# Layer 0 of a hybrid-mixer kernel: the state-space mixer moved behind all projections, beside axial attention

## The chip, the cores and the metric

The kernel runs on one core of a Trainium2 chip. The core has five engines that run at the same time, each with its own queue of instructions that it works through in order: TensorE (matmuls, PE in the profile, with its weight loads as PEld), VectorE (DVE), ScalarE (ACT), GpSimd (POOL) and SyncE (SP, which here only issues DMAs). The metric is the device time of one execution in microseconds, as the median of several runs.

## The reference, cut to what matters

Two layers work on 512 latent and 256 context tokens of width 1024. Each layer projects the normalised tokens once and feeds four parallel mixers; the context is only needed as an output of the first layer (`need_ctx`).

```python
def _layer(x, xc, c, c_ctx, rope, need_ctx, ...):
    ...
    aq, ak, av, dq, dk, dv, fin, sin_ = _split_proj(h @ w_in)
    caq, cak, cav, cdq, cdk, cdv, cfin, csin = _split_proj(hc @ w_in)
    o_a, oc_a = _gqa_mixer(aq, ak, av, caq, cak, cav, att_q_gain, att_k_gain, rope, need_ctx)
    o_d, oc_d = _na_mixer(dq, dk, dv, cdq, cdk, cdv, na_q_gain, na_k_gain, na_rel_bias, need_ctx)
    o_f = _fourier_mixer(fin, w_fourier)
    o_s, oc_s = _s5_mixer(sin_, csin, ssm_lam_re, ssm_lam_im, ssm_log_dt, ..., need_ctx)
    o = _group_norm(jnp.concatenate([o_a, o_d, o_f, o_s.astype(o_a.dtype)], axis=-1), g_group)
    x = x + ga1 * (o @ w_out)
    h2 = _rmsnorm(x, g_norm2) * (1.0 + sc2) + sh2
    x = x + ga2 * _swiglu(h2, w_ff1, w_ff3, w_ff2)
```

`_gqa_mixer` is the axial attention of the change's name (4 heads, rotary positions), `_na_mixer` the near attention (a window with a bias), `_s5_mixer` a state-space scan over the tokens in both directions with a gelu and a gated linear unit at its end.

## The kernel before, in words

The kernel is written in a tile language: the program gives tiles, pools and instructions; a scheduler then orders the instructions of each engine by program order as priority, whether they are ready, and its own clock. An instruction waits for the tiles that it reads and for the release of the space that it writes, be it a buffer of a pool or space that an earlier, closed pool held. SBUF is two stacks: pools opened on the left and on the right (`side="right"`). PSUM has eight banks; in each stage they are given out to roles (`psum_pools`): `D` for dense work, `S` for scores, `Q` for attention's other matmuls, `T` for everything that fills in.

Precision is kept by splitting float32 into a high and a low part: `mm3` (L237) does three matmuls per product, and `weights` (L222) loads a weight group on SP's queue, makes the high part on ScalarE (L231) and the low part on POOL (L232).

`mixers` (L1084) is called once per layer. For layer 0 (l = 0) its program order before the change is:

1. The projections for s5 (`oS`), for the queries and keys of axial attention (`aq`, `ak`), their head statistics, norm and rotary step (L1100 to L1118), in role D, T for the statistics.
2. `before_s5`, which is `tables` (L424): the coefficients of s5, made on VectorE and POOL with small matmuls in role S, stored to DRAM through ScalarE's queue.
3. Inside the pool `s5{l}` (`sp` on the left stack): `s5` (L707) in role S; then the projections DK, DQ (L1126) and V (L1145) in role D.
4. After `sp` is closed: the pools `fo`, `on`, `qk`, `fh` in the same space, the splits `k2`, `q2` of axial attention (L1160), and the F projection (L1170), emptied into `fhi` and `flo` (L1165).
5. The stage `b`, with S = 2 tiles of 1024, Q = 2 and T = 2 banks: `attend` twice (L957), and as fillers in role T `mods_pe` for chunks 4 and 5 (L358), `group_stats` of `oS`, `norm_heads` of near attention, and `fourier` (L829) in a pool `ft` on the left.
6. The stage `c`: near attention (L996), whose bias (`nab`) is loaded on SP's queue (L1197) into the pool `qn`, `mods_pe` for chunks 6 to 9 and the group norms in role T, then the output projection in role D.

`s5` makes two passes (m = 0, 1), each: transposes (L719, L727), a matmul with R per direction (L747), a run of VectorE instructions per direction (L754 to L784, with two scans L765 and the state moves L782, L784), the output matmuls (L799, L801), transposes back (L808) and a gelu (L810). After both, the gated unit: matmuls L819, sigmoid L821, products L827. Its tiles `rr`, `oo`, `toep` share three buffers; the rotation tables `rot` have two. Its loads (R, rot, O, T) are issued on POOL's queue.

`attend` works on blocks of two query tiles: scores (L932) into S, the maximum on VectorE (L972, L973), the exponential on ScalarE (L974), transposes (L979), copies (L982, L984), the values (L990), and the division (L946 to L952).

The pool `ga` of axial attention is opened on the right, where `h`, the input of all projections, was held until the F projection ended.

## Time and profile before

| | us |
|---|---|
| median of three runs | 1827.36 |
| the three runs | 1827.08, 1827.36, 1835.40 |
| the profiled execution, in all | 1835.55 |
| its span, first to last instruction | 1833.8 |
| TensorE busy / VectorE busy / ScalarE busy / POOL busy | 1725.8 / 969.5 / 527.2 / 558.6 |
| mean granted share of TensorE's clock | 0.967 |

All rows are from the one profiled execution; its time is close to the highest of the runs. Times inside a trace are us from the first instruction. Layer 0's mixers lie between about 55 and 440 us of it. A line number is that of the kernel before; a helper's line (L241, L232, L265) stands for all of its callers, and the tile's name tells them apart.

### The profile page before, as it was taken

How to read it: one execution, taken by the hardware profiler on the slowest of the kernel's cores; microseconds unless marked ns; L12 is line 12 of the kernel's file. 1: busy time of each engine (PE TensorE's matmuls, PEld its weight loads, DVE VectorE, ACT ScalarE, POOL GpSimd, SP SyncE). 2: the span in 40 equal slices, each digit the busy share in tenths (PEclk: the TensorE clock that was granted, in tenths of full speed). 3: DMA queues.
4: the chain of work that ended last, by engine and by line, in shares of the span. 5: the costliest groups of instructions: out<-in, count | busy, mean ns of one | idle time of the engine just before them, and what ended most of it. 6: DMA issues, size and time to landing. Idle time of an engine off the chain costs nothing.

```text
span 1833.8 us, 25688 instructions
## 1 busy us (share of the span) xinstructions
PE 1725.8 (94%) x10142; PEld 1395.3 (76%) x10142; DVE 969.5 (53%) x2259; ACT 527.2 (29%) x852; POOL 558.6 (30%) x360
## 2 busy tenths in 40 slices
PE   5899999898999999999899998989999999999999
PEld 2667877566878888888678877778767787787887
DVE  7988535572177445446956346265666632232332
ACT  2422234452241211121121223323444432222221
POOL 4553200201221322231643512423111244344442
PEclk7999989999999999999899998989999999999999
DMA  8355340414135434343342332332322123233222
GB/s 337 103 155 165 128 167 24 167 53 182 38 125 151 127 127 153 107 154 110 106 110 75 106 112 81 132 110 89 114 64 64 47 92 93 77 107 103 93 92 81
DMA packets 83065, 207.25 MB, mean 113 GB/s; under 512 B 15360, under 2 KB 35968, under 8 KB 82816
## 3 DMA queue, kind: packets, MB, share of 16 engines
q1 hardware_dynamic: 54160, 160.44, 26.9%
q0 software_dynamic: 7824, 29.38, 4.8%
q10 hardware_dynamic: 20960, 15.78, 2.8%
q8 instruction: 80, 1.31, 0.3%
q14 instruction: 41, 0.34, 0.1%
HBM read 185.68 MB, written 21.99 MB: 113 GB/s over the span
## 4 chain that ended last, share of the span: by engine, by line
PE 76%; DVE 15%; issue 4%; ACT 2%; POOL 1%; DMA 1%; ACTq 0%; DVEq 0%; POOLq 0%
PE psD L241 54%; PE psD L703 4%; PE psS L932 3%; PE psT L241 2%; PE psQ L979 1%; PE psQ L990 1%; PE psT L376 1%; PE psS L801 1%; POOL lo L232 1%; PE psT L856 1%; PE psQ L1045 1%; DVE ro L662 1%; PE psQ L1030 1%; PE psT L278 1%; PE psT L1067 1%
## 5 line engine op out<-in xcount | busy, mean ns | idle before, releaser
L232 POOL TENSOR_TENSOR lo<-raw,hi 128x1024 fp32r<-128x1024 f32 (+1 forms) x178 | 432.2, 2434 | 875.5 <-ACT hi L231 875.2
L241 PE MATMUL psD<-big,hi 128*128 128x512 f32 (+1 forms) x2368 | 605.9, 360 | 12.2 <-ACT big L331 5.7
L241 PEld LDWEIGHTS psD<-big,hi 128*128 128x128 f32 x2368 | 399.8, 191 | 88.1 <-ACT big L331 8.1
L231 ACT CAST hi<-raw 128x1024 fp32r<-128x1024 f32 (+1 forms) x178 | 184.2, 1039 | 774.5 <-PE psD L241 466.6
L241 PE MATMUL psD<-big,lo 128*128 128x512 f32 (+1 forms) x1184 | 368.2, 359 | 1.2 <-POOL lo L232 1.2
L241 PEld LDWEIGHTS psD<-big,lo 128*128 128x128 f32 x1184 | 202.9, 191 | 38.4 <-POOL lo L232 2.7
L1332 DVE TENSOR_TENSOR sg<-sg,psD 128x768 f32<-128x768 f32 (+1 forms) x44 | 36.1, 820 | 308.8 <-PE psD L241 300.5
L241 PE MATMUL psD<-gh,hi 128*128 128x512 f32 (+1 forms) x528 | 163.6, 359 | 4.9 <-DVE xb L1248 4.7
L241 PE MATMUL psD<-gl,hi 128*128 128x512 f32 (+1 forms) x528 | 165.8, 360 | 0.0
L241 PE MATMUL psD<-gh,lo 128*128 128x512 f32 (+1 forms) x528 | 163.6, 358 | 0.0
L1248 DVE SCALAR_TENSOR_TENSOR xb<-psD,mod,xb 128x512 f32<-128x512 f32 (+1 forms) x112 | 64.7, 613 | 114.9 <-PE psD L241 114.8
L1337 DVE TENSOR_TENSOR gl<-sg,gh 128x768 fp32r<-128x768 f32 (+1 forms) x44 | 99.2, 2254 | 39.5 <-ACT gh L1335 39.5
L407 DVE CUSTOM_DVE_ANT_0 junk<-wmt,cb,pcol 128x1024 f32<-128x1024 f32 x64 | 97.1, 1517 | 27.3 <-DMA wmt<-in_wmodT 26.2
L241 PEld LDWEIGHTS psD<-gh,hi 128*128 128x128 f32 x528 | 89.5, 189 | 24.4 <-DVE xb L1248 8.5
L241 PEld LDWEIGHTS psD<-gh,lo 128*128 128x128 f32 x528 | 90.1, 189 | 16.6 <-issue 0.2
L241 PEld LDWEIGHTS psD<-gl,hi 128*128 128x128 f32 x528 | 89.8, 189 | 15.8 <-issue 0.4
L1248 DVE SCALAR_TENSOR_TENSOR xq<-psD,mod,xq 128x512 f32<-128x512 f32 (+1 forms) x64 | 42.2, 682 | 78.6 <-PE psD L241 78.6
L932 PE MATMUL psS<-k,q 64*128 64x256 f32 (+1 forms) x432 | 78.2, 336 | 3.4 <-DVE mx L1019 3.0
L241 PE MATMUL psD<-h,hi 128*128 128x512 f32 (+1 forms) x288 | 76.2, 350 | 4.2 <-ACT h L331 2.7
L932 PEld LDWEIGHTS psS<-k,q 64*128 64x128 f32 x432 | 58.1, 195 | 23.6 <-issue 9.1
L241 PEld LDWEIGHTS psD<-h,hi 128*128 128x128 f32 x288 | 50.7, 194 | 15.4 <-ACT h L331 3.2
L241 PE MATMUL psD<-on,hi 128*128 128x256 f32 (+1 forms) x176 | 51.6, 331 | 1.3 <-ACT on L1081 1.3
(396 smaller groups left out, 2494.5 us busy)
## 6 DMA issues: line engine op xcount, KB each, us to landing
raw<-in_w_ff SPq DMA_DIRECT2D x132, 512.0 KB, 3.5
wmt<-in_wmodT SPq DMA_DIRECT2D x48, 512.0 KB, 3.6
wm<-in_wmod SPq DMA_DIRECT2D x28, 512.0 KB, 6.0
raw<-in_winT SPq DMA_DIRECT2D x18, 512.0 KB, 3.6
room<-in_wmod SPq DMA_DIRECT2D x12, 512.0 KB, 11.4
nab<-in_nab SPq DMA_DIRECT2D x8, 640.0 KB, 4.2
rot<-trot POOLq DMA_DIRECT2D x8, 576.0 KB, 6.0
cf<-in_four POOLq DMA_DIRECT2D x8, 520.0 KB, 4.9
```

Source lines behind the costliest of these rows:

```text
L231: nc.scalar.copy(hi, raw)
L232: nc.gpsimd.tensor_sub(lo, raw, hi)
L241: nc.tensor.matmul(o, lhsT=lhs[i], rhs=rhs[j][..., s], start=start and n == 0, stop=stop and n == 2)
L278: self.nc.tensor.matmul(dst, lhsT=src, rhs=self.ident, start=True, stop=True)
L376: nc.tensor.matmul(ps[32 * j:32 * j + 32], lhsT=self.cvec[:, k], rhs=ws[k // 2][:, k % 2], start=half == 0, stop=half == 1)
L407: nc.vector.tensor_tensor_reduce(junk, w, cb[:, i], 1.0, self.pcol[1][:, PC_B + f:PC_B + f + 1], op0=ALU.mult, op1=ALU.add, accum_out=mod[ ...
L662: v.tensor_mul(er[:, :, :, o], er[:, :, :, s], bcr)
L703: nc.tensor.matmul(ps, lhsT=h[i][:, k, tk], rhs=w[j][:, k % per], start=k == 0 and q == 0, stop=k == KT - 1 and q == 2)
L932: self.nc.tensor.matmul(dst, lhsT=q2[i][h, qc], rhs=view(k2[j][h]), start=n == 0, stop=n == 2)
L1248: self.nc.vector.scalar_tensor_tensor(x[:, m, sl], ps[:, sl], gate[:, m, i:i + 1], x[:, m, sl], op0=ALU.mult, op1=ALU.add)
L1332: nc.vector.tensor_mul(sg, sg, pp[1])
L1337: marks.append(nc.vector.tensor_sub(gl, sg, gh))
```

## The change

Only `mixers` and `s5` are touched. For layer 0 (`after`), the projections DK, DQ and V are put directly behind `before_s5`; s5 itself is called in stage `b`, ahead of `attend`, in role T; its pool is opened after `fh` and closed before `ft` is opened. The tiles `on` are allocated later, in the space of the closed `qk`; a new pool `qd` takes the place of `qk` for the second pair of heads of near attention. In `s5`, `apart` replaces the four half-tile gelus by copies, and does two whole-tile gelus behind both passes. For both layers, the splits of near attention stand behind the bias loads.

```diff
-    def s5(self, l, us, nt_out, sp, role):
+    def s5(self, l, us, nt_out, sp, role, apart=False):
...
-                nc.scalar.activation(u.rearrange("p (j n) -> p n j", n=8)[:, 4 * x:4 * x + 4], pz[:, :, :96],
-                                     AF.Gelu_apprx_tanh)
-            self.dump(f"gel{l}{m}", u)
+                dst = u.rearrange("p (j n) -> p n j", n=8)[:, 4 * x:4 * x + 4]
+                if apart:
+                    nc.scalar.copy(dst, pz[:, :, :96])
+                else:
+                    nc.scalar.activation(dst, pz[:, :, :96], AF.Gelu_apprx_tanh)
+        for m in range(2):
+            if apart:
+                nc.scalar.activation(us[m], us[m], AF.Gelu_apprx_tanh)
+            self.dump(f"gel{l}{m}", us[m])
...
-        with tc.tile_pool(name=f"s5{l}", bufs=1) as sp:
-            self.s5(l, oS, nq, sp, "S")
-            for i in range(2):
-                self.dump(f"os{l}{i}", oS[i])
+        after = l == 0
+
+        def other_projections():
             for x, (base, dst, gi, n) in enumerate(((T_DK, dk, 3, 6), (T_DQ, dq, 2, nq))):
...
+        def mix_s5(role):
+            with tc.tile_pool(name=f"s5{l}", bufs=1) as sp:
+                self.s5(l, oS, nq, sp, role, after)
+                for i in range(2):
+                    self.dump(f"os{l}{i}", oS[i])
+                if not after:
+                    other_projections()
+
+        if after:
+            other_projections()
+        else:
+            mix_s5("S")
+
...
-        on = [None if k in late else onp.tile([P, nqn], F32R, name=f"on{k}") for k in range(KT)]
+
+        def on_tiles():
+            onp = cl.enter_context(tc.tile_pool(name=f"on{l}", bufs=1))
+            return [None if k in late else onp.tile([P, nqn], F32R, name=f"on{k}") for k in range(KT)]
+
+        on = None if after else on_tiles()
...
+            self.psum_pools(st, f"b{l}", S=(2, 1024), Q=(2, 512), T=(2, 512))
+            if after:
+                mix_s5("T")
             fp = fhs.enter_context(tc.tile_pool(name=f"ft{l}", bufs=1))
-            self.psum_pools(st, f"b{l}", S=(2, 1024), Q=(2, 512), T=(2, 512))
             for i in range(2):
                 self.attend(gpool, q2[i], k2, Vg, (0, 64), nq, aq[i],
...
             fhs.close()
+            if after:
+                qks.close()
+                on = on_tiles()
+                qk = qks.enter_context(tc.tile_pool(name=f"qd{l}", bufs=1))
             qn = qks.enter_context(tc.tile_pool(name=f"qn{l}", bufs=1))
-            k2n, q2n = self.split(qn, dk[0], NT, "k2", 2), self.split(qn, dq[0], nqn, "q2", 2)
...
             G = [bias(qn, s, f"nab{s}") for s in range(2)]
+            k2n, q2n = self.split(qn, dk[0], NT, "k2", 2), self.split(qn, dq[0], nqn, "q2", 2)
```

## Rows read from the trace of the kernel before

**Rows 1.** The page, part 1: busy us, share of the span, instructions.

```profile
PE 1725.8 (94%) x10142; PEld 1395.3 (76%) x10142; DVE 969.5 (53%) x2259; ACT 527.2 (29%) x852; POOL 558.6 (30%) x360
```

**Rows 2.** Busy time by stretch: stretch, length, engines, granted clock, DMA share, GB/s.

```profile
200.00:215.00 15.00, 13.99 (x95) 13.34 (x93) 14.88 (x29) 3.78 (x9) 4.64 (x4) 1.00 0.32 100
215.00:228.00 13.00, 9.45 (x73) 9.48 (x74) 3.96 (x3) 1.19 (x3) 3.04 (x2) 0.87 0.55 224
...
236.50:257.00 20.50, 18.28 (x148) 14.20 (x148) 6.92 (x13) 8.20 (x15) 1.66 (x3) 1.00 0.60 230
```

**Rows 3.** Groups by line on TensorE, 0 to 560: busy us, mean ns | idle before.

```profile
L801 PE MATMUL psS<-oo,hst 128*96 128x128 f32 x64 | 11.3, 296 | 5.5 <-POOL lo L232 4.6 <-DVE hst L784 1.0
...
L799 PE MATMUL psS<-toep,U 128*96 128x128 f32 x32 | 6.7, 293 | 0.0
L747 PE MATMUL psS<-U,rr 128*64 128x96 f32 x128 | 6.2, 249 | 0.0
L819 PE MATMUL psS<-oS,wglu 128*128 128x512 f32 (+1 forms) x16 | 5.7, 487 | 0.0
...
L719 PE MATMUL psS<-cst,oS 128*96 128x128 f32 x16 | 2.4, 274 | 0.0
```

**Rows 4.** Groups by line on VectorE, 128 to 245.

```profile
L782 DVE TENSOR_TENSOR hst<-zt 64x124 f32<-64x124 f32 (+2 forms) x12 | 9.0, 774 | 0.1
...
L765 DVE TENSOR_TENSOR_SCAN zt<-rot,zt 128x384 f32<-128x384 f32 x8 | 7.2, 937 | 0.0
...
L754 DVE TENSOR_TENSOR zt<-psS,rot 128x384 f32<-128x384 f32 x4 | 2.2, 554 | 0.6 <-PE psS L747 0.6
```

**Rows 5.** Timeline of s5, TensorE, VectorE and POOL: start us, us, instruction.

```profile
149.04 2.20 PE L747 MATMUL psS<-U,rr 128*64 128x96 f32 x48
...
203.70 1.25 DVE L782 TENSOR_TENSOR hst<-zt 64x124 f32<-64x124 f32 x4
...
211.98 6.06 POOL L232 TENSOR_TENSOR lo<-raw,hi 128x1024 fp32r<-128x1024 f32 x2 [5.90 <-ACT hi L231]
...
212.66 3.18 DVE L782 TENSOR_TENSOR hst<-zt 64x380 f32<-64x380 f32 x2
...
235.60 1.82 DVE L827 TENSOR_TENSOR oS<-sg,oS 128x768 f32<-128x768 f32 x2 [16.57 <-PE psS L819]
```

**Rows 6.** Busy time by stretch: axial attention, its first part, near attention.

```profile
257.00:367.00 110.00, 105.04 (x764) 76.31 (x764) 62.09 (x152) 47.24 (x101) 10.97 (x6) 0.92 0.31 107
257.00:272.00 15.00, 14.68 (x82) 11.46 (x84) 8.20 (x31) 4.72 (x9) 0.00 (x0) 0.57 0.55 197
350.00:418.00 68.00, 58.28 (x499) 42.28 (x497) 50.90 (x170) 35.42 (x88) 8.18 (x7) 0.97 0.25 81
```

**Rows 7.** Timeline, TensorE and VectorE: the ends of attention and fourier.

```profile
256.93 1.31 PE L932 MATMUL psS<-k,q 64*128 64x512 f32 x12
...
288.44 1.13 PE L844 MATMUL psT<-wf,cst 128*128 128x256 f32 x4
...
327.67 0.49 DVE L883 SCALAR_TENSOR_TENSOR oF<-psT,pp 128x129 f32<-128x129 f32 x2
...
367.41 0.68 DVE L1019 CUSTOM_DVE_ANT_0 pe<-psS,nab 128x512 f32<-128x512 f32 x1
```

**Rows 8.** The page, part 6: DMA issues, KB each, median us to landing.

```profile
nab<-in_nab SPq DMA_DIRECT2D x8, 640.0 KB, 4.2
...
cf<-in_four POOLq DMA_DIRECT2D x8, 520.0 KB, 4.9
```

**Rows 9.** Groups by line on TensorE, 330 to 350.

```profile
L376 PE MATMUL psT<-wm,cvec 128*32 128x512 f32 x64 | 8.5, 597 | 0.0
...
L382 PE MATMUL psT<-cst,stat 128*128 128x2 f32 x32 | 3.9, 247 | 0.0
```

**Rows 10.** Timeline of ScalarE, 176 to 190.

```profile
184.21 1.28 ACT L810 ACT_TABLE_LOAD   x1
```

More of the change, by code (lines that the diff above doesn't have):

```diff
@@ L1145, in mixers @@
             self.proj_tok(ws, 2, h, 6, evac_v, "D")
+        def mix_s5(role):
[9 more added lines that the diff above has]
+            mix_s5("S")
         fo = cl.enter_context(tc.tile_pool(name=f"fo{l}", bufs=1))
         flo = fo.tile([P, nq, 256], F32, name="flo", tag="flo")
-        onp = cl.enter_context(tc.tile_pool(name=f"on{l}", bufs=1))
         late = (2, 3) if x_src is None else (0, 1, 2, 3)
-        on = [None if k in late else onp.tile([P, nqn], F32R, name=f"on{k}") for k in range(KT)]
+        def on_tiles():
+            onp = cl.enter_context(tc.tile_pool(name=f"on{l}", bufs=1))
+            return [None if k in late else onp.tile([P, nqn], F32R, name=f"on{k}") for k in range(KT)]
+        on = None if after else on_tiles()
         x, lows = None, [None] * 4
```

## The prediction

> **What bounds the kernel now.** I read the page first: TensorE is busy 94% of the span and no other engine over 53% [rows 1]. That looks like a kernel with nothing left to hide, so the second view is busy time by stretch, laid over the place of the change in the first layer (0 to 450 us). Two things stand there. Between 200 and 257 us, where the state-space mixer (s5) ends and axial attention has not begun, TensorE is idle for 1.0, 3.6 and 2.2 us, 6.8 us together [rows 2]. Nothing else could be issued: the V projection was done, and the F projection could not be emptied, because fhi and the split tiles are allocated on the left stack where the pool of s5 (`sp`) was still open. And in the attention stretch, 257 to 367 us, TensorE is called busy for 105.0 of 110 us, but VectorE only for 62.1 and ScalarE for 47.2 [rows 6]. The third view is the time of the single steps of s5 (TensorE groups in [rows 3], VectorE groups in [rows 4], its order in [rows 5]): a chain of short matmuls, copies and runs of VectorE instructions. The fourth is the order at the end of attention [rows 7]: the first score matmul starts at 256.93, fourier runs from 288.44 to 328.2 inside attention, and near attention starts its first softmax at 367.41. So between 257 and 367 attention itself ended last; fourier was over 39 us earlier.
>
> **What changes.** Only layer 0 (`after` is l == 0). Layer 1 has the same instructions; only the place of two loads and two splits differs there. No matmul is removed or added. s5 moves from before the DK, DQ, V and F projections to behind them, from the three banks of role S to the two of role T, whose other users (mods_pe, group_stats, norm_heads, fourier) come after it in the program.
>
> **Step 1: attention starts earlier.** What stood on TensorE before 256.93 and goes: five of the seven TensorE groups of s5, 11.3 + 6.7 + 6.2 + 5.7 + 2.4 = 32.3 us [rows 3], and the idle 6.8 us [rows 2], together 39.1. Attention can start at 256.9 - 39.1 = 217.8 us. Ends: 214 if the two small groups (I put them at 4 us in all from their like, L719) go as well, 224 if a fifth of the busy time of these groups was overlapped with projections. I take the weights of the projections to arrive in time as they did before, and the tables, their DMAs on ScalarE's queue and the loads on POOL's queue stay where they are. The loads of s5 on POOL's queue (R, rot, O, T) pass the last weight conversions there; one that waits for h to be released would hold a `lo` behind it, but `lo` of winF is the last of the stage.
>
> **Step 2: s5 in its new place.** Before, it ran from its first matmul with the tables' data (149.04) to its last multiply (235.60 + 1.82 = 237.4): 88.4 us for two passes [rows 5]. In the second pass the four-part state moves took 3.18 us for two instructions while POOL converted weights for 6.06 us at the same time, and 1.25 us for as many elements without it [rows 5]; L784 shows the same, so 2 x 1.9 = 3.9 us go, since POOL has no weights to convert there now. By my count of tile sizes the tiles of s5 beyond R and the first rot (zt, hst, the second rot) lie where h is until the F projection ends, so only the first 2.2 us of matmuls (L747) can be ahead of attention. 88.4 - 3.9 - 2.2 = 82 us; that its VectorE work now queues with attention's, and its matmuls no longer behind dense projections, I set equal. s5 ends at 217.8 + 82 = 299.8. Bounds: VectorE needs 2 x 9.0 + 7.2 + 10 x 2.2 (ten groups like L754) + 1.8 = 49 us for it [rows 4, 5], and with half of its matmuls unhidden (16) the shortest is 65; if every VectorE instruction of the attention stretch queued in front, 49 + 62 = 111 [rows 4, 6].
>
> **Step 3: fourier can't start before s5 ends.** Its pool (ft) now lies in the space of sp. Its first cf load lands 4.9 us after issue [rows 8]: 304.7. Before it took 39.7 us, first matmul to last oF, with all of attention around it [rows 7]; by 300 us about half of that stretch's work is done (82 less the 49 that s5 needs of VectorE leaves 33, of the 62 that the whole stretch took [rows 6]), so I take 33, between 39.7 and an estimate of 28 alone. It ends at 337.7. The near-attention bias lies on ft's end, and lands 4.2 us after issue [rows 8]; a split and a score matmul go beside it and 1 us behind: near attention starts at 343, against 367.4, **-24.5 us**. What is late next is fourier's chain, not attention.
>
> **Step 4: covers that go.** The modulation matmuls of chunks 6 to 9 ran between 330 and 350 inside attention, 8.5 + 3.9 = 12.4 us of TensorE [rows 9]. They wait for the T banks of fourier, so they now fall beside near attention, where TensorE was idle 9.7 of 68 us [rows 6]; such idle pieces are short, so I let a third hide: **+8**. Attention's exponentials now stand around s5's gelu and sigmoid; a table load is 1.28 us [rows 10], and one more at least is needed (exp, gelu, sigmoid, exp), up to six if they interleave: +1.3 to +7.7, taken as two, **+2.6**. The added pair of whole-tile gelus replaces four half ones with copies beside attention: nothing, or 1 us at the end of the chain. Reordering bias and splits moves two loads on SP's queue; they wait for fourier in either order, and what is queued behind them (weights of chunks 6 to 9 and wout) is used behind fourier's end only: 0, at most 2 either way. The granted clock was 0.57, mostly the 1.2 GHz level, in the first 15 us of attention, after the broken 215 to 257 us [rows 2, 6]; that cost 6.5 us. It can go with the hole or come again in the thinner stretch: 0, bounds -6.5 and +6.5.
>
> **Sum:** -24.5 + 8 + 2.6 = -14 us. Against the profiled execution itself (span 1833.8, 1835.55 in all) that gives 1821.5. That execution is like the highest of the three runs shown (1835.4); the other two are at 1827, so for the median I apply the same -14: **1813 us**.
>
> **Is there room on TensorE at all?** The row of the attention stretch has TensorE busy 105.0 of 110 us and weight loads 76.3 [rows 6]; 32 us of s5 do not fit into 5 us of idle time. By the busy time, then, the change is worth the idle 6.8 us alone. The Trainium skill (Trainium Kernel Development and Optimization, Performance Expectations) calls matmul busy time a bad metric, because matmuls are pipelined, and tells to judge by the weight-load share; by that the stretch is 69% full and 32 us fit. The trace leans to the rule: a group like L932 counts the tail of each matmul as busy, and 12 score matmuls took 1.31 us at 256.93 [rows 7]. By the one the sum would be -6.8, by the other it stands.
>
> On the tables the Trainium skill (ScalarE: Activation LUTs, Table sets: the hidden batching unit) advises to do all calls of one set before switching, which speaks against putting gelu and sigmoid inside the exponentials. The trace shows 1.28 us for a load [rows 10], the page about 2.66 with its drain; by the page two loads are 5.3 and the sum -11.4.
>
> **Rivals.** (1) Only the hole is filled: TensorE's busy time is real work, s5 pushes attention and its fillers by as much as it left behind, and only the 6.8 us go: 1827.4 - 6.8 = 1820.5. For it: 105.0 of 110 [rows 6]; against it: VectorE at 56%, weight loads at 69%. (2) Slower: the fillers are shut out. s5 holds both T banks and the space of ft, so that for its whole length only attention stands beside it; both queue on VectorE in order. If s5 takes 110 us and fourier its 39.7, near attention starts at 217.8 + 110 + 4.9 + 39.7 + 5.2 = 377.6, 10.2 later than before, and with step 4 that is +21: 1848. It decides from s5 longer than 82 + 14 = 96 us. For it: 49 + 62 us of VectorE in one stretch; against it: before, a pass of s5 kept to some 45 us behind dense projections. (3) It doesn't do what it says: the scheduler keeps s5's instructions in front or attention's behind them, so that they run one after the other; what the early projections give, the uncovered s5 takes, about 0: 1827.
>
> **How the numbers follow.** A measurement of this kernel can tell about 0.5% (9 us) from no change. Forecast 0.50, with its own range 1795 to 1820 (s5 between 68 and 90); (1) 0.22; (3) 0.09; (2) 0.19, of which the milder half lies between 1827 and 1837. Faster by over 0.5% (under 1818) is the forecast less its edge, plus the rare case that fourier and the clock do better too: 0.54. Within: 0.29. Slower: 0.17. The range takes the forecast from 1795 and reaches into the slower case to 1838.
>
> **What the profile after would show.** Step 1: first L932 of layer 0 at 214 to 224, and no idle of over 2 us on TensorE before it. Step 2: L827 ends 75 to 90 us later, hst moves at 1.25 us. Step 3: cf is issued within 1 us of that, and the first L1019 follows the last L883 by some 5 us, with attention's last L990 earlier. Step 4: L376 of chunks 6 to 9 behind fourier; four or more table loads. I am wrong if TensorE has long idle pieces between 218 and 300 waiting for VectorE, or if the granted clock stays at half there.

## The result: 14 us slower, and the profile after

The changed kernel takes 1843.54 us (median of 11 runs) against 1827.36 us (median of 11); the ratio is 1.0077 with a 95% interval of 1.0053 to 1.0101. So it is slower by about 14 us by the ratio, 16 by the medians, where 14 us less were forecast. The profiled execution took 1845.81 us, its span 1844.0.

The page, part 1, after (busy us, share of the span, instructions), against [rows 1]:

```profile
PE 1728.3 (94%) x10142; PEld 1395.4 (76%) x10142; DVE 958.4 (52%) x2259; ACT 534.3 (29%) x858; POOL 562.4 (30%) x360
```

It tells nothing: TensorE is at 94% in both. The stretches tell more. They are cut at 150 us, at the first score matmul, at the start of near attention and at the first update of the out-projection, which I use as a mark from here on: 450.2 us before, 467.2 after. Columns as in [rows 2]. First three stretches and the sum of the kernel before, then those of the changed one:

```profile
150.00:256.90 106.90, 96.57 (x713) 82.10 (x707) 63.76 (x149) 30.83 (x57) 20.28 (x23) 0.98 0.39 137
256.90:367.40 110.50, 105.14 (x765) 76.40 (x765) 62.43 (x153) 47.24 (x101) 10.97 (x6) 0.92 0.31 106
367.40:450.20 82.80, 74.29 (x573) 53.62 (x574) 47.51 (x192) 33.44 (x84) 2.14 (x4) 0.96 0.33 118
sum 300.20, PE 276.00 PEld 212.12 DVE 173.70 ACT 111.51 POOL 33.39; mean PE 92.00 PEld 70.71 DVE 57.90 ACT 37.17 POOL 11.13
```

```profile
150.00:215.00 65.00, 63.81 (x423) 57.62 (x421) 20.55 (x72) 15.73 (x35) 14.14 (x12) 1.00 0.23 80
215.00:371.50 156.50, 134.59 (x1014) 100.37 (x1016) 91.05 (x222) 66.07 (x126) 11.12 (x23) 0.88 0.37 123
371.50:467.20 95.70, 89.29 (x657) 63.62 (x656) 53.56 (x201) 38.73 (x92) 11.55 (x8) 0.89 0.41 151
sum 317.20, PE 287.69 PEld 221.61 DVE 165.16 ACT 120.54 POOL 36.81; mean PE 95.90 PEld 73.87 DVE 55.05 ACT 40.18 POOL 12.27
```

Read two columns. TensorE's idle time is the length less PE busy: 24.2 us in the sum before, 29.5 after. The hole ahead of attention is gone (10.3 us idle to 1.2), but the stretch of attention and s5 has 21.9 us of idle where attention had 5.4. And the granted clock: the stretch of attention and s5 got 0.88, near attention and what follows 0.89; before it was 0.92 and 0.96. Length times the part not granted is what I call clock lost: 14.3 us in the three stretches before the change, 29.3 after it.

As a plain count, from the start of each execution up to its mark, first before, then after:

```profile
0.00:450.20 450.20, 397.08 (x2725) 294.62 (x2726) 301.16 (x866) 157.27 (x311) 110.61 (x103) 0.94 0.43 149
0.00:467.20 467.20, 407.98 (x2725) 302.38 (x2726) 290.57 (x865) 164.40 (x317) 114.23 (x103) 0.90 0.41 143
```

TensorE did as many matmuls in both, 2725. Of the 17.0 us between the marks, 10.9 are busy time that these matmuls took longer, at a lower clock, and 6.1 are idle time. Behind the mark the changed kernel's profiled execution is 6.8 us shorter than that of the kernel before (1376.8 against 1383.6), so that the two spans differ by 10.2 us only.

How the new stretch runs, from its timeline (columns as in [rows 5]). These answer to [rows 5, 7]; L711 is the first load of s5's pool, L747 its R matmul, L833 its last product (L827 before), L847 the load of fourier's cf, L1025 near attention's first maximum (L1019 before):

```profile
214.33 0.56 POOL L711 DMA_DIRECT2D wglu<-in_wglu  x1 [15.43 <-PE psD L703]
214.95 1.32 PE L938 MATMUL psS<-k,q 64*128 64x512 f32 x12 [0.92 <-DVE flo L1189]
225.74 1.50 PE L747 MATMUL psT<-U,rr 128*64 128x96 f32 x16
324.66 0.95 DVE L833 TENSOR_TENSOR oS<-sg,oS 128x768 f32<-128x768 f32 x1
326.69 1.08 POOL L847 DMA_DIRECT2D cf<-in_four  x2
342.36 1.13 PE L850 MATMUL psT<-wf,cst 128*128 128x256 f32 x4 [0.36 <-DVE dq L948]
371.53 0.69 DVE L1025 CUSTOM_DVE_ANT_0 pe<-psS,nab 128x512 f32<-128x512 f32 x1 [0.21 <-PE psS L938]
```

Attention starts at 214.95, as forecast. But s5 can load nothing before the F projection is done, so its first R matmul comes 10.8 us behind the first score matmul, and its last product ends at 325.6: 100 us for the two passes, 88 before. Then the fillers take the T banks for 16 us, fourier 24, and near attention starts at 371.5, not 24 us earlier than before but 4 later.

The prediction named a granted clock that stays at half between 218 and 300 us as a sign of being wrong. It came in part: the clock was 0.80 from 226 to 262 us, with 7.4 us of TensorE idle, and 0.89 from there to the end of s5:

```profile
226.00:262.00 36.00, 28.65 (x222) 22.80 (x221) 27.24 (x59) 11.17 (x22) 4.27 (x9) 0.80 0.28 91
```

### The profile page after: what moved, and what is told of

It is laid out like the page before. It is cut to its first block, busy times and chain, and to the rows that moved or that the text cites. A ratio compares the mean times of both kernels' runs of the same rounds, so it can differ in the third digit from the quotient of the medians.

```text
span 1844.0 us, 25682 instructions
## 1 busy us (share of the span) xinstructions
PE 1728.3 (94%) x10142; PEld 1395.4 (76%) x10142; DVE 958.4 (52%) x2259; ACT 534.3 (29%) x858; POOL 562.4 (30%) x360
## 4 chain that ended last, share of the span: by engine, by line
PE 75%; DVE 14%; issue 4%; DMA 3%; ACT 2%; POOL 2%; ACTq 0%; POOLq 0%; DVEq 0%
PE psD L241 53%; PE psD L703 4%; PE psS L938 3%; PE psT L241 2%; PE psQ L996 1%; PE psQ L985 1%; DMA cf<-in_four 1%; PE psQ L1051 1%; PE psQ L1036 1%; PE psT L265 1%; DVE q L661 1%; PE psT L862 1%; PE psT L376 1%; DVE ro L662 1%; POOL lo L232 1%
## 5 line engine op out<-in xcount | busy, mean ns | idle before, releaser
L241 PEld LDWEIGHTS psD<-h,hi 128*128 128x128 f32 x288 | 50.3, 192 | 16.1 <-ACT h L331 3.2
## 6 DMA issues: line engine op xcount, KB each, us to landing
room<-in_wmod SPq DMA_DIRECT2D x12, 512.0 KB, 11.4
```

Of the source, the lines that this page charges most:

```text
L241: nc.tensor.matmul(o, lhsT=lhs[i], rhs=rhs[j][..., s], start=start and n == 0, stop=stop and n == 2)
```

## The experiments

All kernels were timed in turns with the kernel before; the ratio is to it, with its 95% interval. Starts, ends and marks are from the one profiled execution of each. Such a number scatters: the kernel below with its gelus in halves has the median of the changed kernel within 1 us (1844.10, 1843.54), but reaches the mark at 458.4 us where the changed kernel's profile has 467.2; and the first score matmul of the kernel with the bias order alone changed came at 263.3 us instead of 256.9, while its mark did not move (450.8). A difference of less than some 9 us between two such numbers is therefore not shown by them.

### What s5 costs in either place

**s5 left out of the kernel before:**

```diff
-            self.s5(l, oS, nq, sp, "S")
+            if l:
+                self.s5(l, oS, nq, sp, "S")
```

> The kernel before with s5 of layer 0 left out (its transposes, matmuls, scans, gelu and gated unit; its tables are still made), so that the difference to the kernel before is what s5 costs in its old place. Theory now held (s5 is a chain of about 80 us that TensorE has 30 us of work in; in the old place all of it but the hole and its own matmuls is covered by the projections): it costs 32.3 us of matmuls in full and 6.8 us of hole, 36 to 46 us, and the time is 1784 to 1794. Rival (the projections' busy time has room for s5's matmuls): it costs only its hole and its last matmuls, 10 to 25 us, and the time is 1805 to 1820.

**s5 left out of the changed kernel**, by the same condition in `mix_s5`:

> The changed kernel with s5 of layer 0 left out, likewise: the difference to the changed kernel is what s5 costs in its new place. Theory (in the new place the fillers wait for the end of a chain of 100 us, so that the chain and not TensorE's work is paid for): 48 to 65 us, 10 to 20 us more than in the old place, and the time is 1778 to 1796, about that of the kernel before without s5. Rival (s5 costs the same in either place, and the loss is in what else was changed: the order of the projections, the late tiles, the mods beside near attention): the cost is within 5 us of that in the old place, and the changed kernel without s5 is 10 to 18 us slower than the kernel before without s5.

Measured: 1806.53 us, 0.9894 (0.9856 to 0.9932), for the old place, and 1793.23 us, 0.9817 (0.9781 to 0.9852), for the new. The stretches of the two (150 to first score, to near attention, to the mark), first without s5 from the kernel before, then from the changed one:

```profile
150.00:220.50 70.50, 69.18 (x448) 58.82 (x448) 20.38 (x73) 17.21 (x36) 15.54 (x13) 1.00 0.29 103
220.50:325.30 104.80, 102.45 (x780) 71.66 (x780) 57.81 (x154) 48.08 (x102) 8.14 (x5) 0.97 0.34 126
325.30:417.80 92.50, 82.08 (x575) 60.23 (x576) 50.14 (x193) 34.70 (x86) 4.52 (x5) 0.87 0.33 116
sum 267.80, PE 253.72 PEld 190.71 DVE 128.33 ACT 99.99 POOL 28.20; mean PE 84.57 PEld 63.57 DVE 42.78 ACT 33.33 POOL 9.40
```

```profile
150.00:225.50 75.50, 74.18 (x463) 63.20 (x462) 23.54 (x77) 18.15 (x38) 17.06 (x12) 0.98 0.28 99
225.50:331.10 105.60, 103.41 (x781) 71.84 (x780) 57.93 (x155) 48.48 (x103) 8.19 (x5) 0.97 0.30 111
331.10:416.80 85.70, 79.02 (x574) 58.22 (x574) 48.74 (x192) 34.15 (x85) 4.53 (x5) 0.88 0.37 127
sum 266.80, PE 256.61 PEld 193.27 DVE 130.22 ACT 100.77 POOL 29.78; mean PE 85.54 PEld 64.42 DVE 43.41 ACT 33.59 POOL 9.93
```

This is the pair on which the rest stands. Without s5 both profiled executions reach the mark at about the same time, 417.8 and 416.8: there the order of the projections, the late tiles and the bias order show no cost. With s5 the marks are 450.2 and 467.2. So by the marks s5 costs 32.4 us in the old place and 50.4 in the new. Of that, idle TensorE is 24.2 - 14.1 = 10.1 in the old and 29.5 - 10.2 = 19.3 in the new; clock lost is -0.9 and +14.3 us, by the price found below (0.68 us for each) -0.6 and +9.7. What is left is 22.9 and 21.4 us, which I put down to s5's matmuls: about the same in either place. (This counts from 150 us. In the old place some of s5's first matmuls lie before that; counted from the start of the execution, the same working leaves 26 and 28 us.) And the attention stretch by itself, with nothing of s5 on VectorE, takes 105 us with TensorE idle for 2.3: by its busy time it was full.

The medians say 21.7 us for the old place and 50.3 for the new; by the ratios it is 19 and 48. The first is lower than by the marks, and the lower clock of that kernel's four runs can explain it: their mean is 0.9625 against 0.9703 in the kernel before, that is 13.6 us of clock lost more, some 9 us of time by the price below. By the ratios the changed kernel without s5 is even 0.8% faster than the kernel before without it, and its profiled execution (1802.54 us) was the slowest of its four. So the rest of the change does not cost the 14 us; what costs them is s5 in its new place, 18 us dearer by the marks and 28 by the ratios. The expectation of 36 to 46 us for the old place was too high by its matmuls: 32.3 us by [rows 3], where 22 to 27 of busy time were added. A sum over groups counts time twice where matmuls of two groups overlap; in the changed kernel's stretch from 215.0 to 371.5 the groups by line add up to 155 us, and TensorE was busy for 134.6.

**s5 by itself, ahead of attention:**

```diff
+            if after:
+                with ExitStack() as s5st:
+                    self.psum_pools(s5st, f"a{l}", U=(1, 512), T=(2, 512))
+                    mix_s5("T")
             self.psum_pools(st, f"b{l}", S=(2, 1024), Q=(2, 512), T=(2, 512))
-            if after:
-                mix_s5("T")
```

> The changed kernel with one edit: s5 of layer 0 has its two T banks in a stage of its own, over the banks of the scores, so that attention can't start until s5's last matmul is emptied. Theory (s5 is a chain that is long by itself; attention adds 10 to 20 us to it): from its first R matmul to its last product it takes 72 to 82 us here, against 100 in the changed kernel and 88 in the kernel before; attention starts at about 300 and has all its fillers beside it, near attention starts at about 405 (371.5 in the changed kernel), and the time is 25 to 35 us above the changed kernel. Rival (VectorE, queued with attention, is what made it 100): 50 to 62 us by itself, attention starts at about 285, the time 10 to 18 us above.

Measured: 1858.26 us, 1.0169 (1.0141 to 1.0197). R matmul at 222.7, last product ending at 290.6: 68 us, between the two expectations and nearer to the first. Attention adds 32 us to it, more than the 10 to 20 that I gave it. What TensorE waited for in that stretch (engine, waiting line, releaser: us in total, times, longest):

```profile
PE psT L799 <- DMA toep<-tt: 9.3, 1, 9.3
PE psT L799 <- DVE zt L755: 7.1, 1, 7.1
PE psT L747 <- DMA rr<-tr: 6.3, 2, 3.8
PE psT L801 <- issue: 5.2, 2, 4.9
```

So s5 is a chain with 28 us of waits of its own in these four rows, and near attention came at 392.4. Against that, the changed kernel is 21 us ahead at this point and some 15 to 17 in its time: s5 beside attention does save something, only less than the projections had saved.

### Is it the queue behind s5?

**Chunks 4, 5 and norm_heads ahead of s5** (and taken from behind `attend`):

```diff
             if after:
+                self.mods_pe((4, 5), "T")
+                norms()
                 mix_s5("T")
```

> One edit against the changed kernel: in stage b of layer 0, the modulation chunks 4 and 5 and the four norm_heads of near attention stand ahead of s5 in the program, no longer behind it. Theory (shut-out fillers): s5 holds the T banks for about 110 us, and what stood behind it runs bare between its last product (325.6 us) and fourier's first matmul (342.4). Of these 16.8 us, 9 to 12 go, because the fillers now use the 11 us in which s5 waits for its loads; near attention starts at about 361 instead of 371.5, and the time is 8 to 11 us below the changed kernel (1833 to 1836, about 1.004 of the kernel before). Rival (s5's own length beside attention is all that matters, the fillers are short work that only shifts): s5 starts later by what they take, and the time moves by less than 3 us (1841 to 1846).

Measured: 1843.35 us, 1.0075 (1.0056 to 1.0094). The rival held: the first R matmul moved from 225.7 to 244.9, the last product to 335.6, near attention to 367.7.

**Fourier ahead of s5 too:**

```diff
+                oF = fourier()
+                fhs.close()
                 mix_s5("T")
```

> Against the changed kernel: chunks 4 and 5, norm_heads and fourier stand ahead of s5 in stage b of layer 0, so that s5 takes the space of the closed ft. Theory (shut-out fillers): fourier runs beside attention from 218 to about 258, s5 from there beside the rest of attention, in 80 to 90 us since half of attention's VectorE work is over, and ends at 340 to 350. Near attention starts at about 350 instead of 371.5, the time falls by 15 to 22 us, to 1821 to 1828, and the ratio to the kernel before is 0.996 to 1.001. Rival (s5 beside attention takes its 100 us wherever it starts, because VectorE and the half clock set it): s5 ends at 358 or later, near attention starts at 362, and the time is at most 10 us below the changed kernel (1833 or more).

Measured: 1847.94 us, 1.0087 (1.0063 to 1.0111). Fourier ran from 238.9 to 273.0, s5 from 280.7 to 359.3, near attention from 368.2; again the rival. In the second pass attention's maxima were done (307.8) and still TensorE waited:

```profile
PE psT L799 <- DMA toep<-tt: 7.3, 1, 7.3
PE psT L801 <- issue: 4.4, 1, 4.4
```

**Five buffers for R, O and toep in that kernel** (`bufs=3` to `bufs=5`):

> Against the run with fourier ahead of s5 (ratio 1.0087): R, O and toep of s5 in layer 0 share five buffers instead of three, so that all loads of a pass are issued at its start. Theory (s5 is slow by its own chain of loads: in the second pass TensorE stood 7.3 us waiting for toep, which had waited for R's buffer): that wait goes in both passes, s5's last product comes at 345 to 352 instead of 359.3, near attention starts at 354 to 361 instead of 368.2, the ratio is 1.002 to 1.006. Rival (the loads are waited for beside VectorE's chain, which is as long): the last product comes less than 4 us earlier and the ratio is 1.007 to 1.010.

Measured: 1848.04 us, 1.0100 (1.0075 to 1.0125); last product 360.9, near attention 369.9. The rival held. The wait of 7.3 us stayed (7.1, now put down to "issue"), so the shared buffers were not what held toep back.

**s5's first tiles below h:**

```diff
+        low = qks.enter_context(tc.tile_pool(name=f"s5low{l}", bufs=1)) if after else None
         qk = qks.enter_context(tc.tile_pool(name=f"qk{l}", bufs=1))
...
-                r = sp.tile([P, 4, 2, P], F32, name="rr", tag="ro", bufs=3)
+                r = low.tile([P, 4, 2, P], F32, name="rr", **two)
```

> Against the changed kernel: the tiles that s5 needs first (uy, U, R with toep in a ring of two, the rotation tables) lie in a pool of their own ahead of qk on the left stack, below the space of h, so that their loads and s5's first transposes needn't wait for the F projection's last matmul; the O tiles keep a ring of two in the late pool. Theory (the changed kernel's s5 began 10.8 us behind the first score matmul because its whole pool lay where h was, and the chain is on the path that ends last): the first R matmul comes before 212 instead of at 225.7, s5's last product at 311 to 317 instead of 325.6, near attention starts at 357 to 363 instead of 371.5, and the time is 8 to 13 us below the changed kernel, ratio to the kernel before 1.000 to 1.004. Rival (two T banks and VectorE's queue set the pace of s5 beside attention, so an earlier start is waited away): the last product comes less than 5 us earlier, ratio 1.005 to 1.008.

Measured: 1845.99 us, 1.0095 (1.0067 to 1.0123). The first R matmul came at 203.2 and the last product at 313.6, 12 us earlier, as the theory said. Near attention started at 366.1, only 5.4 earlier, and the time did not fall at all; neither expectation held in full. Attention's first transposes waited 8.2 us for their exponential, and from s5's end to fourier's first matmul on its input (340.2 here, 343.1 in the changed kernel) it was 26.6 us instead of 17.5.

**The fillers moved off the T banks, on top of that:**

```diff
             if after:
+                self.mods_pe((4, 5), "Q")
+                norms()
                 mix_s5("T")
```

with `norms` in role S, and `group_stats` behind fourier.

> Against the run with s5's first tiles below h (s5's last product at 313.6, fourier's first matmul at 340.2, near attention from 366.1, ratio 1.0095): chunks 4 and 5 take the banks of role Q ahead of attention, the four norm_heads those of role S ahead of attention, and group_stats of oS stands behind fourier, so that nothing but fourier stands behind s5 in the two T banks. Theory (one queue: s5, the fillers and fourier go one after the other through the T banks, and near attention starts when that queue is through): of the 26.6 us between s5's last product and fourier's first matmul 16 to 20 go (a load of cf, 5 us, and its own first copies stay), near attention starts at 347 to 354, and the ratio to the kernel before is 0.998 to 1.003, unless the clock takes it back. Rival (the fillers ahead only push s5 and attention by as much as they took behind it, as chunks 4, 5 and the norms did once before, so that TensorE's work is the bound): s5's last product comes at 325 or later, near attention starts within 5 us of 366, ratio 1.006 to 1.010.

Measured: 1847.67 us, 1.0109 (1.0085 to 1.0132). The same matmul of fourier came 2.3 us after s5's last product (322.5 and 320.2), as wanted, and near attention still started at 366.1, as the rival has it: attention itself began at 243.5 instead of 215 and had its last values at 363.4, and fourier, now with attention beside it, took 38 us instead of 24. The stretches of this kernel:

```profile
150.00:243.50 93.50, 86.42 (x656) 72.99 (x654) 42.44 (x119) 19.43 (x41) 20.89 (x20) 1.00 0.44 159
243.50:366.10 122.60, 108.08 (x772) 84.53 (x772) 69.91 (x170) 63.88 (x121) 5.69 (x12) 0.89 0.16 53
366.10:467.50 101.40, 95.80 (x681) 64.77 (x681) 55.00 (x216) 40.64 (x95) 12.06 (x8) 0.88 0.45 159
```

Five orders of the same work (the changed kernel's and four others), and near attention starts at 371.5, 367.7, 368.2, 366.1 and 366.1. So the queue behind s5 is not what holds it. In each, TensorE's work stands with some 22 us of idle around it (7.1 + 14.5 here, 1.2 + 21.9 in the changed kernel), wherever the pieces stand, and what I gained at one place came back at the next. That TensorE's work is the bound is argued from this and not shown: no run took these 22 us away. No kernel of this study beats the kernel before, but for those that leave work out.

### The other parts of the change

**Early projections alone, s5 ahead of F in role S** (with the whole-tile gelus and the bias order kept, and without the call in stage `b`):

```diff
             other_projections()
-        else:
-            mix_s5("S")
+        mix_s5("S")
```

> Against the changed kernel: s5 is back ahead of the F projection, in role S and on the left stack ahead of fo, but DK, DQ and V still stand ahead of it in the program. So the early projections are tried alone. Theory (what the projections hid is what the move gives up): s5 has only the V projection and the end of DQ beside it, ends at about 240, TensorE has a hole of 20 to 40 us before the F projection, attention starts at 265 to 280 and has its fillers beside it again; near attention starts at 375 to 390, and the time is 8 to 22 us above the kernel before (1835 to 1850). Rival (the order of the projections is of no weight, as s5 is a chain of waits either way): s5 ends at 237 as before, and the time is within 4 us of the kernel before.

Measured: 1846.06 us, 1.0084 (1.0065 to 1.0103), in the theory's range. s5's last product came at 262.1, even later than the 240 expected, attention at 281.6 and near attention at 386.5, since hardly more than the V projection was left to run beside s5. The projections are s5's cover; putting them first uses it up.

**Gelus per half again** (`self.s5(l, oS, nq, sp, role)`):

> Against the changed kernel: the four half-tile gelus stand again where the kernel before had them, inside the two passes, and the copies that replaced them are gone. Theory (shut-out fillers): the activation tables are no term of the loss; one or two more loads of 1.28 us on ScalarE, the time within 4 us of the changed kernel (1840 to 1848). Rival (the tables make s5 long): seven loads stand in the stretch of attention and s5 of the changed kernel; gelus between the exponentials add at least two loads in each pass, which stand in s5's chain and in attention's, and the time grows by 6 to 12 us (1850 to 1856). If the split itself cost time, it would fall by 3 us or more.

Measured: 1844.10 us, 1.0069 (1.0046 to 1.0093), as the changed kernel. Table loads in the stretch rose from seven to nine, 1.28 us each, without a difference in time that can be told. No run took the seven away.

**Bias ahead of splits in the kernel before** (the two lines exchanged):

> The kernel before with only the splits of near attention put behind the bias loads, in both layers, as the change does. Theory (this part is of no weight): layer 0's out-projection and layer 1's first scores come within 2 us of the kernel before, ratio 0.998 to 1.002. Rival (the bias loads get ahead of weights on the one load queue, and the second layer pays for it): 3 to 8 us more, ratio 1.002 to 1.004.

Measured: 1830.52 us, 1.0016 (1.0000 to 1.0032); mark 450.8 against 450.2. The ratio is in the theory's range, and its interval reaches into the rival's, up to some 6 us. It is no large part of the loss.

**Only the hole filled: F's tiles below s5's pool in the kernel before:**

```diff
+        if early:
+            fo, flo = open_f()
+            fh = cl.enter_context(tc.tile_pool(name=f"fh{l}", bufs=1))
         with tc.tile_pool(name=f"s5{l}", bufs=1) as sp:
...
             self.proj_tok(ws, 2, h, 6, evac_v, "D")
-
...
+            if early:
+                f = project_f(fh)
```

> The kernel before with one thing moved: in layer 0 the tiles of the F projection (flo, fhi) lie below s5's pool, so that the F projection needn't wait until s5 is done; s5 stays in its old place. It fills the hole that the change was to fill, without putting s5 beside attention. Theory (the hole, 6.8 us between 200 and 257, is all that the old place left to gain): attention starts at 250 to 254 instead of 256.9, and the ratio to the kernel before is 0.996 to 0.999. Rival (the hole is not the F projection's: s5's end itself, and the splits behind it, hold attention): attention starts at 256 or later, ratio 0.999 to 1.002.

Measured: 1835.20 us, 1.0039 (1.0016 to 1.0061): above both ranges. Attention starts at 258.5, but in this execution s5's first R matmul also came 4.2 us later (153.3 against 149.0), so this start decides for neither side. Counted from that matmul attention starts 2.6 us earlier, and near attention starts at 363.7, 3.7 us earlier than before; neither is clear of the scatter. What followed was slower: from its first maximum to its last near attention was granted 0.73 of the clock, where the kernel before got all of it (first this kernel, then the kernel before):

```profile
363.70:421.60 57.90, 52.93 (x354) 41.78 (x353) 38.02 (x144) 27.29 (x65) 2.36 (x1) 0.73 0.19 57
367.40:411.70 44.30, 40.52 (x352) 30.79 (x353) 35.38 (x143) 25.74 (x63) 0.00 (x0) 1.00 0.18 55
```

Over all its runs it lost 61.5 us of clock against 54.2 in the kernel before; by the price below that is 5 of the 7 us. Of the waits between 200 us and the start of attention one is left:

```profile
PE psS L801 <- POOL lo L232: 4.6, 1, 4.6
```

The kernel before has the same row. So 4.6 of the 6.8 us of the hole [rows 2] were never the F projection's. The row names POOL, whose conversion ended at 218.0 in the kernel before. But this matmul reads what s5's own state moves write, and it started at 218.55, right behind one of them:

```profile
215.87 2.58 DVE L784 TENSOR_TENSOR hst<-zt 64x380 f32<-64x380 f32 x1
```

These moves are slow while POOL converts weights [rows 5].

### The displaced modulation chunks

**Chunks 6 to 9 left out, of the changed kernel and of the kernel before:**

```diff
-                self.mods_pe(range(6, 10), "T")
+                nc.vector.memset(self.mod[0][:, 24:40], 0.0)
+                self.gain_scale(0, 1)
```

> The changed kernel with the modulation chunks 6 to 9 left out (their values are set to zero), so that the difference to the changed kernel is what they cost beside near attention. Theory (they cost all their TensorE time there, and the half-clock piece beside them): near attention from its first to its last maximum takes 44 to 48 us instead of 56, and the time is 10 to 16 us below the changed kernel. Rival (near attention is slower because of the clock alone): 52 us or more, the time at most 6 us lower.

> The kernel before with the modulation chunks 6 to 9 left out likewise. Theory (in the old place they lay in the end of attention and were partly covered): near attention starts 3 to 8 us earlier than 367.4, and the time is 3 to 8 us below the kernel before, 5 to 10 less than the same cut brings the changed kernel. Rival (no cover there either, TensorE's work counts in full): 10 to 14 us.

Measured: 1837.84 us, 1.0046 (1.0031 to 1.0061), and 1817.36 us, 0.9941 (0.9923 to 0.9958). They cost the kernel before 12.0 us, the changed one 1.0077 - 1.0046 = 0.0031, some 6 us, give or take 5 by the two intervals. By the times both rivals held: no cover in the old place, and half of one in the new. (Near attention did shrink to the 46 us of the theory, 380.5 to 426.8, but it started 9 us later, with more clock lost ahead of it.) So the displacement shows as no term of the loss.

**Chunks 6 to 9 in the Q banks behind s5**, on the kernel with fourier first:

> Against the run with fourier ahead of s5 (1847.9): the modulation chunks 6 to 9 stand behind s5 in stage b, in the two banks of role Q, which attention has given back by 314 us, and no longer beside near attention. Theory (the chunks lost their cover when they fell beside near attention): they run at 315 to 350 in the idle time of s5's second pass, near attention takes 51 us from its first maximum to its last division as in the kernel before, against 61, and the time falls by 7 to 11 us, to 1835 to 1841 by this batch. Rival (they only move TensorE's work from one place that has room to another): s5's second pass is stretched by the same 8 to 12 us, near attention starts at 377 instead of 368, and the time stays within 3 us of that run.

Measured: 1853.88 us, 1.0141 (1.0118 to 1.0163). They ran at 321 to 381, their loads beside s5's (toep's wait grew from 7.3 to 9.4 us), and near attention, from 369.3, took longer, not less. Neither expectation held: the time rose by some 10 us.

**Chunks 6 to 9 between s5's passes**, on the kernel with the fillers off the T banks (`between()` after m = 0):

> Against the run before it (fillers off the T queue: near attention from 366.1, out-projection's first update at 467.5, ratio 1.0109): the modulation chunks 6 to 9 stand between the two passes of s5, in the T banks, no longer beside near attention. Theory (the stretch up to near attention is bound by TensorE's and VectorE's work together with 20 us of idle pieces that short work can use, and the displaced chunks cost their full length beside near attention): near attention starts at 366 to 373, it takes 50 to 55 us instead of 58 to its last maximum, the first update comes at 456 to 462, ratio 1.004 to 1.008. Rival (s5's chain sets the stretch): the chunks between the passes lengthen the chain by their 13 us and more, near attention starts at 378 to 385, and the ratio stays at 1.009 to 1.013.

Measured: 1853.73 us, 1.0134 (1.0107 to 1.0162). Near attention from 374.2, 8 us later, the mark at 464.3: between the two expectations in the trace, and just above the rival's range in the time.

### The clock

Each timed run comes with its span and mean granted clock. Around each kernel's own means, over 197 runs of 20 kernels, a run that lost 1 us more of full clock (span times the part not granted) was 0.68 us longer, with a correlation of 0.78. That is the price used above; it is a correlation between runs, not an experiment. The kernel before lost 54.2 us on average (0.9703), the changed one 65.6 (0.9644). At 0.68 that would be 7.8 of the 13.7 us between their mean spans. To see whether the clock follows TensorE's use, work was added that computes nothing.

**One useless matmul ahead of each PSUM tile of s5 and attention (T and Q), and of s5's alone (T):**

```diff
+        if role in self.idle_work:
+            k = self.idle_work[role]
+            for _ in range(1):
+                self.nc.tensor.matmul(t[:, :512], lhsT=k[:, :P], rhs=k[:, P:P + 512], start=True, stop=True)
```

> The changed kernel with useless work added: ahead of what is computed in each PSUM tile of s5 (role T) and of axial attention's transposes, values and sums (role Q) in layer 0, one matmul of 128 by 512 from k2's high part is written to the same tile, and overwritten. Over 90 matmuls of 0.25 to 0.45 us, 23 to 40 us of TensorE work, in a stretch with 22 us of idle TensorE. Theory (the clock: TensorE, thinly used beside s5, is granted the half level for 34 us of this stretch and that costs about 8 us of the 14): the granted clock of the stretch from the first score matmul to near attention rises from 0.88 to 0.95 or more, so that the added work is half paid back: 0 to 10 us above the changed kernel. Rival (the clock of the stretch isn't set by how thinly TensorE is used here): it stays at 0.90 or below, and the added work costs 12 to 30 us.

> The same with s5's tiles in role T alone: some 30 to 50 added matmuls, 8 to 20 us of TensorE work, most of it where s5 waits for its loads or for VectorE. Theory (the clock): the granted clock of the stretch rises to 0.91 to 0.95, the time is within 5 us of the changed kernel, on either side. Rival: the clock stays at 0.89 or below and the time is 6 to 15 us above.

Measured: 1853.75 us, 1.0127 (1.0106 to 1.0147), and 1844.42 us, 1.0079 (1.0059 to 1.0099). The attention stretch of the first:

```profile
214.90:372.70 157.80, 145.30 (x1097) 105.59 (x1096) 91.74 (x222) 68.18 (x128) 10.80 (x23) 0.97 0.36 123
```

and the added matmuls in it (line, operation, tiles, shape, count, busy us, mean ns, then the idle time ahead):

```profile
L220 PE MATMUL psQ<-k 128*128 128x512 f32 x50 | 25.3, 511 | 1.8 <-DVE pT L995 1.0 <-ACT pT L993 0.8
L220 PE MATMUL psT<-k 128*128 128x512 f32 x26 | 13.3, 517 | 5.2 <-DVE zt L760 2.1 <-DVE U L735 1.2 <-ACT uy L725 0.9
```

The granted clock of the stretch was 0.97 with these 76 added matmuls, 0.90 with 26 and 0.88 in the changed kernel. But the kernel with its gelus in halves, which adds none, got 0.92:

```profile
215.40:366.60 151.20, 129.97 (x1015) 96.10 (x1016) 91.14 (x223) 67.12 (x126) 11.19 (x23) 0.92 0.38 128
```

So 26 show nothing, and only the 0.97 stands above the other orders of this work (0.88 to 0.94), in one execution. There the clock seems to follow TensorE's use. The two groups of added matmuls come to 38.6 us, but much of that overlaps with others: TensorE's busy time of the stretch rose by 10.7 us (134.59 to 145.30), its idle time fell from 21.9 to 12.5, and the stretch grew by 1.3 us. That execution took 1844.24 us in all, 9.5 below the median of its kernel. The time did not fall: the first kernel is 9 us above the changed one by its ratio, the second as fast, both as their theories allowed; the clock of the second, 0.90, lies between its two expectations. So the changed kernel does get a lower clock, but adding work is no way to gain by it, and why its clock fell stays open.

## Why the prediction was wrong, point by point

- **Step 1** held: 214.95 against 217.8, and no idle above 2 us on TensorE ahead of it. One half of it failed: I let the first R matmuls run ahead of attention. The whole pool waited for h, as the row with 15.43 us shows, and 10.8 us went there.
- **Step 2** failed in its size. Forecast 82 us and an end at 299.8; it was 100 us and 325.6. The state moves came down as forecast, the pair of 64x380 from 3.18 to 1.10 us, though on a misread row: the 1.25 us of the forecast are four moves of 124 elements, 496 against 760 and not "as many". What I set equal was not: beside attention s5 takes 100 us, by itself 68. The prediction's own point from which rival (2) decides was 96 us.
- **Step 3** held as a chain (cf issued 1 us behind s5, near attention 5 us behind fourier, attention's last values at 333.4 before it), and fourier took 24 us, less than the 33 forecast. But 16 us of fillers stood between s5 and fourier, which it forgot. Added up, near attention came 28.5 us later than the forecast 343: s5's end 25.8, the fillers about 12, fourier 9 less. More than that, its question was wrong: five orders of the work gave nearly the same start of near attention.
- **The step that failed** is the one on room. I read 105.0 busy of 110 us, and 69% of weight loads, and chose the second, so that s5's 32 us would fit and the -24.5 us stand. They did not fit: with s5 taken out the stretch still took 105 us with TensorE idle for 2.3, s5's matmuls cost some 22 us (26 to 28 counted from the start) in either place, and near attention came 4 us later instead of 24.5 earlier. The Trainium skill (Trainium Kernel Development and Optimization, Performance Expectations) calls matmul busy time a bad metric for how close a kernel is to roofline. I used that sentence for the room in one stretch, and there the measurement went with the busy time. Busy time is no plain sum all the same: the groups of [rows 3] sum to 32.3 us, of which less was paid, and 38.6 us of added matmuls made the stretch 1.3 us longer in one execution and the kernel 9 us slower by its ratio.
- **Step 4:** the displaced chunks were put at +8 and cost less than before; the tables at +2.6, of which only two further loads were tried, without a difference; the clock at 0 with bounds of 6.5, and it cost about 8 by the price above. That last one was called open and then left at nothing. Where the prediction takes 5.3 us for two table loads, its sum should read -11.2, not -11.4.
- **Rivals:** the direction was that of (2), with its mechanism half right: s5 over its 96 us and the fillers shut out, but taking the fillers from behind it did not help. (1), only the hole filled, is right that TensorE's work moves along and wrong on the sum: the hole closed, and 16.5 us of idle (5.4 to 21.9) and the lower clock opened elsewhere.

The account up to the mark, +17.0 us in the two profiled executions: idle +5.3, clock lost +15.0 at 0.68 = +10.2, together 15.5. By direct count it is 6.1 of idle and 10.9 of longer matmuls. What stays open is why the clock fell, what keeps some 22 us of TensorE idle in every order, and why added work with a higher clock in one execution doesn't bring the time down.

## What to carry to other kernels

A latency chain needs cover that leaves its engines alone: dense projections gave s5 some of its waits for free. Beside attention, which uses VectorE, ScalarE and short matmuls as well, it took 100 us where it takes 68 alone. Before moving work into a stretch whose TensorE is busy for 95% of the time, leave the work out once in both places: the two differences price the move, and here they were 32 and 50 us by the marks. If several orders of the same work end at the same time, stop sorting and look for work to remove.

## What the hardware showed that I had not expected

The granted clock differed by order and by execution: the stretch of attention and s5 got 0.88 to 0.94 of it in the orders that were tried, and 0.97 in the one execution in which 76 matmuls of 0.51 us were added and which made the stretch 1.3 us longer. And a POOL conversion slows VectorE's moves beside it: in the kernel before, a pair of state moves took 3.18 us beside the conversion of 6.06 us [rows 5], and the matmul that reads the moves waited 4.6 us, most of the hole ahead of attention. In the changed kernel no conversion stands there, and the same pair took 1.10:

```profile
300.71 1.10 DVE L782 TENSOR_TENSOR hst<-zt 64x380 f32<-64x380 f32 x2
```

That wait is gone in the changed kernel, and stays when only the F projection is moved.
